# Gate projections ahead of the S5 output steps, and a second norm begun sooner with three up blocks

## The chip, the cores and the metric

The kernel runs on one core of one Trainium2 chip, as one launch. The metric is the device time of that launch in microseconds. Five engines work side by side, each through its own list of instructions in order: TensorE (PE in the profile; PEld is its loading of weights), VectorE (DVE), ScalarE (ACT), GpSimd (POOL) and SyncE (SP), which here only issues DMAs. They wait for one another by semaphores.

## The reference

One layer of a hybrid decoder trunk, in fp32: 256 prompt tokens and 8 x 4 decode tokens, 2048 features.

```python
mod = silu(c) @ W_ada + b_ada        # shift1, scale1, gate1, shift2, scale2, gate2
h = rmsnorm(x) * (1 + scale1) + shift1
q, k, v, g, a_lr, u = split(h @ W_in)
# GLA: 4 heads, dk 128, dv 256; log a = logsigmoid(a_lr W_a2 + b_a2) / 16
S_t = diag(a_t) S_{t-1} + k_t^T v_t;  o_t = q_t S_t;  o = headnorm(o) * silu(g)
# S5: 64 groups of 16 channels, a complex diagonal state of 64 per group
s_t = Abar s_{t-1} + Bbar u_t;  y_t = Re(C s_t) + D u_t
z = gelu(y) * sigmoid(gelu(y) @ W_glu + b_glu)
x = x + gate1 * (concat[o, z] @ W_out)
h = rmsnorm(x) * (1 + scale2) + shift2
x = x + gate2 * ((gelu(a') * g') @ W_down)   # [a' | g'] = causal conv3(h @ W_up), 5632 wide each
y = rmsnorm(x)                               # the final norm
```

The new GLA, S5 and convolution states are outputs too.

## The kernel before

All 288 tokens lie on the free axis (32 decode tokens, then 256 of the prompt), the features on the 128 partitions. A weight block of 128 x 1024 comes by SP's DMA queue into a `raw` buffer, of which there are ten. `split` makes two halves of it for precision: `wh`, a cast on ScalarE (L128), and `wl`, the remainder, a subtraction on VectorE (L130). `mm3` multiplies each 128 x 128 tile three times into one PSUM block `acc`: wh with the activations' high part (L145), wh with their low part (L146), wl with the high part (L147). `proj2(m)` is the second half (8 of 16 feature tiles, 24 matmuls) of output block m of the in-projection; VectorE adds it to the first half, which stands in SBUF.

The adaLN vectors (`mod`) are computed in units of 16 matmuls of 512 columns each (L197, `ada_mms`), straight from four raw buffers of the weight `wadf` each. `step(ada_b, 1)` and `step(ada_g2, 1)` put half a unit's work between other blocks; `chained` binds a unit's matmuls to one another and to `tail`, the last matmul of the block before. A scheduler sets the order of the instructions on every engine from the program's order, priorities (loads and splits run ahead) and data dependences; `after` adds an order by hand.

The stages on the time axis: adaLN and in-projection, S5 preparation, the projections m = 8 to 23 beside the chunked attention, the S5 outputs with the projections m = 24 to 31 (which hold g, the gate of the GLA output), the GLA state update, the GLU, the out-projection ("mixer blocks", `mixo`, `x2`), the second norm, then up projection, convolution and down projection, and the final norm.

**S5 outputs.** The state `st` holds every fourth token after a scan on POOL: a step of four operations (L725 to L728) for each, one behind the other. For each f of 0 to 7, `advance` makes the tokens between (two products into `q`, L678, and two additions into `st`, L679, on VectorE for even f and on POOL for odd). 48 small matmuls into two PSUM tiles follow (L880 with `MM` and `UU`, L882 with `st`), copies on ScalarE into `zt` (L885), four transposes (L888) and a copy on VectorE (L890). Then comes projection 24 + f, whose result VectorE adds to `PG` (L894).

**GLA state.** The prompt's state is formed by the matmuls L922 and stored from tile `S11` to `o_glap` (L924, POOL's queue). The decode states come in pieces by loads from `sgla` (L949, same queue) into `S10`, `S11` (S in the profile) and `MM`, and are multiplied with the queries (L954). S11 is free for its load when the store has landed, MM when the last S5 output has read its matrix.

**Second norm.** The squares of x are summed up in `ssq` beside the mixer blocks; two matmuls with ones add `ssq` and the last `sq` (L1095, L1096), `rms_rstd` makes the scale `rst` (L156 to L161). Then, for pieces of 1, 1, 2, 4, 4 and 4 of the 16 feature tiles, x is multiplied with `rst` (L1104, the last two pieces on POOL), the decode tokens get their shift (L1106), ScalarE writes the high part `hh` (L1111, L1112) and VectorE the low part `hl` (L1117, L1119). `up_mm2` runs the first two up blocks together, a feature tile at a time, as its pieces come (L1156 to L1158).

## Time and profile before

| what | value |
|---|---|
| three runs | 1476.24, 1483.79, 1479.89 us; median 1479.89 |
| the profiled execution | 1480.4 us; its span 1478.5 us |
| PE busy | 1407.0 us, 95% of the span |
| DVE, ACT, POOL busy | 910.8, 677.7, 346.5 us |
| PE idle between 330 and 430 us | 14.8 us in one wait, about 7 in smaller ones |
| PE idle between 592 and 606 us | 3.02, 1.01, 2.56, 0.70 us |
| moved by DMA | 317 MB, 214 GB/s on the mean |

Times in a trace count from the start of the span. In the prediction's rows from the timeline stand the start, the duration, the engine, the line, the operation, output <- inputs by the program's names (buffer numbers left out) and the count; in brackets the idle time of the engine before it and what ended it. In rows of stretches stand the bounds, the length, the busy time and number of instructions of PE, PEld, DVE, ACT and POOL, then the granted clock of PE (1.00 is full), the DMA's busy share and its GB/s. Matmuls overlap in the pipeline, so their starts tell their pace.

### The profile page before, as it was taken

The numbers are of one execution on the slowest core, as the hardware profiler recorded it, in microseconds if no ns is written. First come the engines' busy times: TensorE is split into PE (matmuls) and PEld (weight loads), VectorE is DVE, ScalarE is ACT, GpSimd is POOL, SyncE is SP. The second block draws the span as 40 slices with busy tenths as digits, with TensorE's granted clock in tenths as the row PEclk, the third lists the DMA queues.
The fourth block names the chain that finished last, engine by engine and source line by source line (L and its number), as shares of the span: only waits on it lengthen the run. The fifth ranks groups of instructions, "written<-read, shape, count | busy, mean of one in ns | idle before, by whom it ended". The sixth has DMA issues, their size and how long they took to land.

```text
span 1478.5 us, 28963 instructions
## 1 busy us (share of the span) xinstructions
PE 1407.0 (95%) x11546; PEld 1298.6 (88%) x11546; DVE 910.8 (62%) x1643; ACT 677.7 (46%) x1131; POOL 346.5 (23%) x618
## 2 busy tenths in 40 slices
PE   5999999995999999899999999999999999999996
PEld 4777777774778988789999999999999999999995
DVE  6866573582366856755665666565655665666557
ACT  4651254334344445544435543554345534553445
POOL 1126013496211001332103320232023301330121
PEclk9999999998999999899999999999999999999998
DMA  9977978882679776678444445544544454445432
GB/s 374 336 270 224 357 272 289 280 285 88 246 272 376 270 274 239 251 274 295 161 169 167 162 147 183 170 160 154 177 166 168 160 171 159 170 160 169 148 103 79
DMA packets 88727, 316.96 MB, mean 214 GB/s; under 512 B 10368, under 2 KB 10784, under 8 KB 88592
## 3 DMA queue, kind: packets, MB, share of 16 engines
q1 hardware_dynamic: 84240, 299.72, 58.1%
q0 software_dynamic: 4064, 14.81, 2.9%
q8 instruction: 91, 1.49, 0.4%
q10 hardware_dynamic: 288, 0.59, 0.1%
q14 instruction: 44, 0.36, 0.1%
HBM read 306.63 MB, written 8.45 MB: 213 GB/s over the span
## 4 chain that ended last, share of the span: by engine, by line
PE 71%; POOL 4%; DMA 2%; DVE 2%; issue 1%; ACT 0%; DVEq 0%; SPq 0%; POOLq 0%; ACTq 0%
PE acc L145 22%; PE acc L146 22%; PE acc L147 22%; PE ada L197 2%; POOL q L726 1%; POOL st L728 1%; POOL q L725 1%; POOL st L727 1%; DMA raw<-wup 1%; PE s L882 1%; DMA MM<-sgla 1%; DMA o_glap<-S 1%; DMA S<-sgla 0%; PE gl L954 0%; DVE S L1106 0%
## 5 line engine op out<-in xcount | busy, mean ns | idle before, releaser
L128 ACT CAST wh<-raw 128x1024 fp32r<-128x1024 f32 (+1 forms) x376 | 386.0, 1030 | 570.5 <-PE acc L146 510.8
L130 DVE TENSOR_TENSOR wl<-raw,wh 128x1024 fp32r<-128x1024 f32 (+1 forms) x376 | 458.8, 1222 | 278.6 <-ACT wh L128 264.9
L145 PE MATMUL acc<-hh,wh 128*128 128x288 f32 x1376 | 407.7, 296 | 0.0
L146 PE MATMUL acc<-hl,wh 128*128 128x288 f32 x1376 | 405.9, 295 | 0.0
L147 PE MATMUL acc<-hh,wl 128*128 128x288 f32 x1376 | 404.4, 294 | 0.0
L145 PEld LDWEIGHTS acc<-hh,wh 128*128 128x128 f32 x1376 | 257.8, 187 | 4.2 <-ACT up L1167 4.2
L147 PEld LDWEIGHTS acc<-hh,wl 128*128 128x128 f32 x1376 | 259.1, 188 | 0.0
L146 PEld LDWEIGHTS acc<-hl,wh 128*128 128x128 f32 x1376 | 258.3, 188 | 0.0
L1168 POOL COPY cvo<-up 128x16 f32<-128x16 f32 x88 | 101.7, 1156 | 591.7 <-ACT up L1166 591.7
L146 PE MATMUL acc<-ffhl,wh 128*128 128x288 f32 x704 | 208.1, 296 | 0.0
L147 PE MATMUL acc<-ffhl,wl 128*128 128x288 f32 x704 | 207.6, 295 | 0.0
L145 PE MATMUL acc<-ffhl,wh 128*128 128x288 f32 x704 | 207.1, 296 | 0.5 <-ACT ffhl L1198 0.2
L145 PE MATMUL acc<-h,wh 128*128 128x288 f32 x512 | 158.4, 310 | 2.2 <-DVE PG L612 1.2
L147 PE MATMUL acc<-h,wl 128*128 128x288 f32 x512 | 152.9, 301 | 2.7 <-DVE wl L130 2.7
L146 PE MATMUL acc<-h,wh 128*128 128x288 f32 x512 | 153.7, 301 | 1.4 <-DVE h L477 0.9
L146 PEld LDWEIGHTS acc<-ffhl,wh 128*128 128x128 f32 x704 | 132.7, 188 | 0.1
L145 PEld LDWEIGHTS acc<-ffhl,wh 128*128 128x128 f32 x704 | 131.8, 188 | 0.9 <-ACT ffhl L1198 0.5
L147 PEld LDWEIGHTS acc<-ffhl,wl 128*128 128x128 f32 x704 | 132.0, 188 | 0.0
L1044 DVE SCALAR_TENSOR_TENSOR x<-acc,mod,x 128x256 f32<-128x256 f32 x128 | 61.6, 481 | 101.6 <-PE acc L147 101.4
L145 PEld LDWEIGHTS acc<-h,wh 128*128 128x128 f32 x512 | 97.7, 191 | 23.4 <-issue 9.9
L197 PE MATMUL ada<-raw,cS 128*32 128x512 f32 (+1 forms) x832 | 101.3, 569 | 5.0 <-DMA raw<-wadf 3.0
L147 PEld LDWEIGHTS acc<-h,wl 128*128 128x128 f32 x512 | 97.5, 191 | 3.9 <-DVE wl L130 3.4
(416 smaller groups left out, 1963.6 us busy)
## 6 DMA issues: line engine op xcount, KB each, us to landing
raw<-wup SPq DMA_DIRECT2D x176, 512.0 KB, 3.6
raw<-wadf SPq DMA_DIRECT2D x128, 512.0 KB, 6.6
raw<-wdn SPq DMA_DIRECT2D x80, 512.0 KB, 3.5
raw<-wadb SPq DMA_DIRECT2D x48, 512.0 KB, 7.0
raw<-win SPq DMA_DIRECT2D x32, 512.0 KB, 5.7
raw<-winc SPq DMA_DIRECT2D x32, 512.0 KB, 5.5
raw<-wout SPq DMA_DIRECT2D x32, 512.0 KB, 7.8
raw<-wad SPq DMA_DIRECT2D x16, 512.0 KB, 8.9
```

The lines of the kernel that those rows point to most:

```text
L128: cast[0] = S.copy(wh, raw)
L130: V.tensor_sub(wl, raw, wh.bitcast(F32))
L145: T.matmul(ps, wh[:, ks], xh(k), start=first, stop=False)
L146: T.matmul(ps, wh[:, ks], xl(k), start=False, stop=False)
L147: tail[0] = T.matmul(ps, wl[:, ks], xh(k), start=False, stop=last).ins
L197: mms.append(lambda c=c, kc=kc_of(blk, j), raw=raw, c0=c0, first=first, last=last: T.matmul(ps[32 * c:32 * c + 32, 0:w], cS[:, kc, :], raw ...
L725: G.tensor_tensor(q1, prev, a8[:, 0], op=ALU.mult)
L726: G.tensor_tensor(q2, prevs, a8[:, 1], op=ALU.mult)
L727: G.tensor_tensor(cur, cur, q1, op=ALU.add)
L728: G.tensor_tensor(cur, cur, q2, op=ALU.add)
L1044: V.scalar_tensor_tensor(x2[:, m, ND:], ps[:, ND:], mod[:, vi, m, 0:1], x2[:, m, ND:], op0=ALU.mult, op1=ALU.add)
L1168: G.tensor_copy(cvo[:, m, 0:16].rearrange("p (b w) -> p b w", w=2), upd[:, :, 4:6])
```

## The change

The loop over f runs four steps further and is shifted: projections 24 to 27 come before the first S5 output (`s5_out`), and each output f stands behind projection 28 + f, as long as there is one. VectorE's `advance` is ordered behind the addition of the projection before it, and an output's first matmul behind the last matmul before it.

In the second norm one adaLN unit stands ahead of the sum of squares, which is bound to it; four stay behind. All scaling is on VectorE, in pieces of 1, 1, 2, 2, 2, 4 and 4. The weights of three up blocks are loaded and split ahead (their pool has four buffers, not two), and `up_mm_first` runs three blocks together, the third in a PSUM tile `gl`: for each feature tile the six matmuls with hh, then the three with hl. In the final norm two scratch tiles come from another pool.

```diff
-        def advance(eng, dst, src, srcs, fs, n):
+        def advance(eng, dst, src, srcs, fs, n, prev=None):
...
+                if prev is not None and w_ == 0:
+                    order_after(ins.ins, prev)
                 eng.tensor_tensor(dst, dst, q, op=ALU.add)
...
-        for f in range(8):
+        def s5_out(f):
             fs = slice(4 * f, 4 * f + 4)
             advance(G if f % 2 else V, ...
-                    fs, 31)
+                    fs, 31, None if f % 2 else gadd[0])
...
+                    if al_ == 0 and j == 0:
+                        order_after(mm0.ins, tail[0])
...
-            ps = proj2(24 + f)
-            V.tensor_add(proj_dst(24 + f), ps, proj_dst(24 + f))
-            step(ada_b, 1)
+        for f in range(8 + 4):
+            if f < 8:
+                ps = proj2(24 + f)
+                gadd[0] = V.tensor_add(proj_dst(24 + f), ps, proj_dst(24 + f)).ins
+                step(ada_b, 1)
+            if f >= 4:
+                s5_out(f - 4)
...
+        keep_tail[0] = True
+        step(ada_g2, 1)
+        keep_tail[0] = False
         psn = ps_gl()[:, 0:NT]
-        T.matmul(psn, ones, ssq, start=True, stop=False)
-        T.matmul(psn, ones, sq, start=False, stop=True)
+        for i, t in enumerate((ssq, sq)):
+            ins = T.matmul(psn, ones, t, start=(i == 0), stop=(i == 1))
+            order_after(ins.ins, tail[0])
+            tail[0] = ins.ins
...
-        parts = ((0, 1), (1, 1), (2, 2), (4, 4), (8, 4), (12, 4))
+        parts = ((0, 1), (1, 1), (2, 2), (4, 2), (6, 2), (8, 4), (12, 4))
...
-            (V if k0 < 8 else G).tensor_tensor(t, t, rst..., op=ALU.mult)
+            V.tensor_tensor(t, t, rst..., op=ALU.mult)
...
-    wpools.append(ctx.enter_context(tc.tile_pool(name="wspb", bufs=2)))
-    up_w = [[f() for f in load_w(a["wup"][i])] for i in range(2)]
-    step(ada_g2, 5)
+    wspb = ctx.enter_context(tc.tile_pool(name="wspb", bufs=4))
+    wpools[:] = [wspb] * 4 + [wspa] * 2
+    up_l = [load_w(a["wup"][i]) for i in range(3)]
+    up_w = [[None, None] for _ in range(3)]
+    for i, hf in ((0, 0), (1, 0), (2, 0), (0, 1), (1, 1), (2, 1)):
+        up_w[i][hf] = up_l[i][hf]()
+    wpools[:] = [wspb, wspa, wspb]
+    step(ada_g2, 4)
...
+        pss = [ps_acc(), ps_acc(), ps_gl()[:, 0:NT]]
         for k in range(KC):
-            for i in range(2):
+            ks = slice(k % 8 * P, (k % 8 + 1) * P)
+            for i in range(3):
                 wh, wl = up_w[i][k // 8]
                 T.matmul(pss[i], wh[:, ks], hh[:, k], start=(k == 0), stop=False)
-                T.matmul(pss[i], wh[:, ks], hl[:, k], start=False, stop=False)
-                T.matmul(pss[i], wl[:, ks], hh[:, k], start=False, stop=(k == KC - 1))
+                T.matmul(pss[i], wl[:, ks], hh[:, k], start=False, stop=False)
+            for i in range(3):
+                wh, wl = up_w[i][k // 8]
+                tail[0] = T.matmul(pss[i], wh[:, ks], hl[:, k], start=False, stop=(k == KC - 1)).ins
```

On VectorE, at the end of the attention and the first S5 output, before the change: the addition of the last v projection, a weight split, the four state operations of output 0, then the copies and additions of the next steps.

```order
L864 TENSOR_TENSOR PV_31_296<-acc_4176,PV_31_296 128x288
L130 TENSOR_TENSOR wl_4338<-raw_4246,wh_4336 128x1024
L678 TENSOR_TENSOR q_4202<-st,a_2335 128x248
L678 TENSOR_TENSOR q_4205<-st,a_2335 128x248
L679 TENSOR_TENSOR st<-st,q_4202 128x2x4x31
L679 TENSOR_TENSOR st<-st,q_4205 128x2x4x31
L915 TENSOR_TENSOR PT_802_4869<-gl_4894,PT_802_4869 32x512
L890 COPY UU_699_4242<-tr_4237 128x4x72
```

After it (L910 is the addition to PG, L684 and L687 are the state operations, L903 the copy):

```order
L910 TENSOR_TENSOR PG_32_297<-acc_4290,PG_32_297 128x288
L130 TENSOR_TENSOR wl_4368<-raw_4362,wh_4366 128x1024
L910 TENSOR_TENSOR PG_32_297<-acc_4336,PG_32_297 128x288
L130 TENSOR_TENSOR wl_4456<-raw_4364,wh_4454 128x1024
L910 TENSOR_TENSOR PG_33_298<-acc_4370,PG_33_298 128x288
L684 TENSOR_TENSOR q_4412<-st,a_2335 128x248
L684 TENSOR_TENSOR q_4415<-st,a_2335 128x248
L687 TENSOR_TENSOR st<-st,q_4412 128x2x4x31
L130 TENSOR_TENSOR wl_4532<-raw_4526,wh_4530 128x1024
L687 TENSOR_TENSOR st<-st,q_4415 128x2x4x31
L903 COPY UU_732_4452<-tr_4447 128x4x72
```

Five splits and five additions now stand between the last v projection and the state operations, and a split between the two additions into `st`.

On PE at the load into S11 (S_818; gl_4945 collects the decode tokens' outputs), before: the transposes of output 4 follow, and then a projection.

```order
L954 MATMUL gl_4945<-S_818_4951,PV_814_4933 32x256 x2
L954 MATMUL gl_4945<-S_817_4950,PV_814_4933 32x256 x2
L954 MATMUL gl_4945<-S_818_4951,PV_814_4933 32x256 x2
L880 MATMUL s_764_4629<-MM_1538,UU_473_2818 72x64
L888 MATMUL tr_4565<-ident,zt_4536 128x72 x4
L145 MATMUL acc_4580<-h_1807,wh_4576 128x288
```

After, with output 5 right behind them:

```order
L972 MATMUL gl_4945<-S_818_4951,PV_814_4933 32x256 x2
L972 MATMUL gl_4945<-S_817_4950,PV_814_4933 32x256 x2
L972 MATMUL gl_4945<-S_818_4951,PV_814_4933 32x256 x2
L891 MATMUL s_781_4747<-MM_1538,UU_473_2818 72x64
L901 MATMUL tr_4733<-ident,zt_4704 128x72 x4
L891 MATMUL s_782_4748<-MM_1538,UU_473_2818 72x64
L895 MATMUL s_781_4747<-cA,st 72x64 x2
```

No projection is left to stand between the outputs 4 to 7; they have all gone ahead. Before the last prompt-state matmul stand three outputs now, as before, but all but one of the projections.

On PE at the second norm, before (a unit is four of the rows L197, one for each raw buffer; the last row is the first up matmul):

```order
L197 MATMUL ada_6954<-raw_6955,cS 32x512 x2
L197 MATMUL ada_6954<-raw_6977,cS 32x512 x2
L197 MATMUL ada_6954<-raw_6975,cS 32x512 x2
L197 MATMUL ada_6954<-raw_6973,cS 32x512 x2
L1095 MATMUL gl_6853<-PT_914_5544,ones 128x288
L197 MATMUL ada_6954<-raw_6971,cS 32x512 x2
L1096 MATMUL gl_6853<-sq_6848,ones 128x288
L197 MATMUL ada_6954<-raw_6993,cS 32x512 x2
L197 MATMUL ada_6954<-raw_6991,cS 32x512 x2
L197 MATMUL ada_6954<-raw_6989,cS 32x512 x2
L197 MATMUL ada_6954<-raw_6987,cS 32x512 x2
L1156 MATMUL acc_7013<-hh,wh_6934 128x288
```

After:

```order
L203 MATMUL ada_6853<-raw_6854,cS 32x512 x2
L1117 MATMUL gl_6870<-PT_914_5544,ones 128x288
L1117 MATMUL gl_6870<-sq_6848,ones 128x288
L203 MATMUL ada_6853<-raw_6993,cS 32x512 x2
L203 MATMUL ada_6853<-raw_6991,cS 32x512 x2
L203 MATMUL ada_6853<-raw_6989,cS 32x512 x2
L203 MATMUL ada_6853<-raw_6987,cS 32x512 x2
L203 MATMUL ada_6853<-raw_7009,cS 32x512 x2
L203 MATMUL ada_6853<-raw_7007,cS 32x512 x2
L203 MATMUL ada_6853<-raw_7005,cS 32x512 x2
L203 MATMUL ada_6853<-raw_7003,cS 32x512 x2
L1184 MATMUL acc_7029<-hh,wh_6963 128x288
```

The sum of squares has moved ahead by nearly a unit; three units stand ahead of the first up matmul as before, two of them behind the sum.

More of the change, by code (lines that the diff above doesn't have):

```diff
@@ L137, in tile_hybrid_step @@
     tail = [None]
+    keep_tail = [False]
     def mm3(ps, w, xh, xl, nk, start, stop):
@@ L166, in after, with order_after @@
     def after(ins, prev):
-        tc.add_manual_dep(ins.ins, prev.ins.name, mybir.DependencyInfo(
+        order_after(ins.ins, prev.ins)
+    def order_after(ins, prev):
+        tc.add_manual_dep(ins, prev.name, mybir.DependencyInfo(
             mybir.DependencyClass.NoSync, mybir.DependencyReason.DATA), reason="order on the engine")
@@ L178, in chained @@
             last = ins.ins
+        if keep_tail[0]:
+            tail[0] = last
     def ada_mms(ps, w, blks, nblk, load, kc_of):
@@ L677, in advance @@
                     "p (r a c) -> p r a c", r=2, a=4)
-                eng.tensor_tensor(q, x, a4[:, w_, :, fs].unsqueeze(3).to_broadcast([P, 2, 4, n]), op=ALU.mult)
+                ins = eng.tensor_tensor(q, x, a4[:, w_, :, fs].unsqueeze(3).to_broadcast([P, 2, 4, n]), op=ALU.mult)
+                if prev is not None and w_ == 0:
+                    order_after(ins.ins, prev)
                 eng.tensor_tensor(dst, dst, q, op=ALU.add)
@@ L867, in tile_hybrid_step @@
         ybuf = []
-        for f in range(8):
+        gadd = [None]
+        def s5_out(f):
             fs = slice(4 * f, 4 * f + 4)
             advance(G if f % 2 else V, st[:, :, fs, NB + 3::2], st[:, :, fs, NB + 2:NCOL:2], st[:, ::-1, fs, NB + 2:NCOL:2],
-                    fs, 31)
+                    fs, 31, None if f % 2 else gadd[0])
             zt = t2k.tile([P, 512], F32, tag="t2k", name=nm("zt"))
@@ L879, in tile_hybrid_step @@
                     o = pzs[j][:, al_ * 64:(al_ + 1) * 64]
-                    T.matmul(o, ut[f][js, al_], mm_[js, pr], start=True, stop=False)
+                    mm0 = T.matmul(o, ut[f][js, al_], mm_[js, pr], start=True, stop=False)
+                    if al_ == 0 and j == 0:
+                        order_after(mm0.ins, tail[0])
                     for r in range(2):
@@ L1099, in tile_hybrid_step @@
         hl = epa.tile([P, KC, NT], F32R, tag="CA", name="hl")
-        parts = ((0, 1), (1, 1), (2, 2), (4, 4), (8, 4), (12, 4))
+        parts = ((0, 1), (1, 1), (2, 2), (4, 2), (6, 2), (8, 4), (12, 4))
         def n2_scale(k0, n):
             t = xa[k0 // 4][:, k0 % 4:k0 % 4 + n]
-            (V if k0 < 8 else G).tensor_tensor(t, t, rst.unsqueeze(1).to_broadcast([P, n, NT]), op=ALU.mult)
+            V.tensor_tensor(t, t, rst.unsqueeze(1).to_broadcast([P, n, NT]), op=ALU.mult)
             td = t[:, :, 0:ND]
@@ L1148, in up_mm, with up_mm_first @@
         return ps
-    def up_mm2(m):
-        pss = [ps_acc(), ps_acc()]
+    def up_mm_first():
+        pss = [ps_acc(), ps_acc(), ps_gl()[:, 0:NT]]
         for k in range(KC):
-            for i in range(2):
+            ks = slice(k % 8 * P, (k % 8 + 1) * P)
+            for i in range(3):
                 wh, wl = up_w[i][k // 8]
-                ks = slice(k % 8 * P, (k % 8 + 1) * P)
                 T.matmul(pss[i], wh[:, ks], hh[:, k], start=(k == 0), stop=False)
-                T.matmul(pss[i], wh[:, ks], hl[:, k], start=False, stop=False)
-                T.matmul(pss[i], wl[:, ks], hh[:, k], start=False, stop=(k == KC - 1))
+                T.matmul(pss[i], wl[:, ks], hh[:, k], start=False, stop=False)
+            for i in range(3):
+                wh, wl = up_w[i][k // 8]
+                tail[0] = T.matmul(pss[i], wh[:, ks], hl[:, k], start=False, stop=(k == KC - 1)).ins
         return pss
@@ L1182, in tile_hybrid_step @@
             if i == 0:
-                pss = up_mm2(0)
+                pss = up_mm_first()
                 ca = up_conv(0, pss[0])
@@ L1186, in tile_hybrid_step @@
             else:
-                ca = up_conv(2 * i, up_mm(2 * i))
+                ca = up_conv(2 * i, pss[2] if i == 1 else up_mm(2 * i))
                 step(ada_g2, 1)
@@ L1227, in tile_hybrid_step @@
     rst = ffp.tile([P, NT], F32, name="rst3")
-    rt1 = ffp.tile([P, NT], F32, name="rt1c")
-    rt2 = ffp.tile([P, NT], F32, name="rt2c")
+    rt1, rt2 = [sml2.tile([P, NT], F32, tag="ft", name=nm("rt")) for _ in range(2)]
     rms_rstd(psn, rst, rt1, rt2)
```

## The prediction

> **What bounds the kernel now.** I read the page's busy shares first, then the waits of TensorE, then the timeline of the two places that the change touches, and last the other engines there. The page:
>
> ```profile
> PE 1407.0 (95%) x11546; PEld 1298.6 (88%) x11546; DVE 910.8 (62%) x1643; ACT 677.7 (46%) x1131; POOL 346.5 (23%) x618
> ```
>
> TensorE (PE) is busy for 1407.0 us, 95% of a span of 1478.5 (the table above): no order of the same matmuls can win more than its 71 idle us and what it loses at a low clock. Two waits of PE between 330 and 430 us (total, times, longest), and ten microseconds of that stretch:
>
> ```profile
> PE s L882 <- DVE st L679: 14.8, 1, 14.8
> PE gl L954 <- DMA S<-sgla: 0.9, 1, 0.9
> ...
> 350.00:360.00 10.00, 5.13 (x57) 4.48 (x58) 2.50 (x5) 1.88 (x5) 9.17 (x20) 0.58 0.01 5
> ```
>
> The first S5 output step waits 14.8 us for VectorE's state addition L679. The granted clock (third number from the end) has fallen meanwhile: 0.58 on the mean of this stretch. Who is late is seen on POOL and DVE:
>
> ```profile
> 332.84 0.34 POOL L725 TENSOR_TENSOR q<-st,a 128x64 f32<-128x64 f32 x1
> 335.77 1.31 POOL L725 TENSOR_TENSOR q<-st,a 128x64 f32<-128x64 f32 x1
> 338.21 0.35 POOL L725 TENSOR_TENSOR q<-st,a 128x64 f32<-128x64 f32 x1
> 339.69 0.35 POOL L725 TENSOR_TENSOR q<-st,a 128x64 f32<-128x64 f32 x1
> ...
> 332.73 0.46 DVE L864 TENSOR_TENSOR PV<-acc,PV 128x288 f32<-128x288 f32 x1 [0.18 <-PE acc L147]
> 335.65 1.23 DVE L130 TENSOR_TENSOR wl<-raw,wh 128x1024 fp32r<-128x1024 f32 x1 [2.47 <-ACT wh L128]
> 352.87 0.90 DVE q L678 x2
> 354.87 0.75 PE L882 MATMUL s<-cA,st 64*72 64x64 f32 x8 [14.82 <-DVE st L679]
> 357.97 0.76 PE L906 MATMUL gl<-ident,PV 128*32 128x128 f32 x4
> ```
>
> POOL's serial scan (L725 to L728, 1.48 us a step from 338.21 to 339.69) ends at 352.85; VectorE's four state operations follow, and PE starts at 354.87. The weight split L130 stretches the scan operation beside it from 0.35 to 1.31 us; the addition out of PSUM at 332.73 leaves its neighbour at 0.34. The second place is the second norm:
>
> ```profile
> 586.32 3.63 PE L197 MATMUL ada<-raw,cS 128*32 128x512 f32 x28
> 591.54 0.75 PE L1096 MATMUL gl<-sq,ones 128*128 128x288 f32 x2
> 595.31 1.93 PE L197 MATMUL ada<-raw,cS 128*32 128x512 f32 x16 [3.02 <-DMA raw<-wadf]
> 598.25 0.53 PE L1156 MATMUL acc<-hh,wh 128*128 128x288 f32 x2 [1.01 <-ACT hh L1112]
> 601.34 0.61 PE L1157 MATMUL acc<-hl,wh 128*128 128x288 f32 x1 [2.56 <-DVE hl L1119]
> 605.28 0.61 PE L1157 MATMUL acc<-hl,wh 128*128 128x288 f32 x1 [0.70 <-DVE hl L1119]
> 610.73 0.38 PE L1156 MATMUL acc<-hh,wh 128*128 128x288 f32 x1
> ...
> 598.00:600.00 2.00, 0.53 (x2) 0.30 (x2) 1.97 (x2) 0.71 (x2) 2.00 (x1) 1.00 1.02 412
> 602.00:604.00 2.00, 2.00 (x10) 2.00 (x10) 1.98 (x4) 1.03 (x3) 0.00 (x0) 0.50 1.04 424
> 612.00:614.00 2.00, 2.00 (x18) 2.00 (x17) 0.85 (x1) 1.94 (x2) 0.38 (x2) 1.00 0.47 83
> ...
> 595.38 2.51 DVE L1106 TENSOR_TENSOR S<-S,mod 128x32 f32<-128x32 f32 x1
> 601.99 0.23 DVE L1106 TENSOR_TENSOR S<-S,mod 128x64 f32<-128x64 f32 x1
> 610.71 0.28 DVE L1119 TENSOR_TENSOR hl<-S,hh 128x128 fp32r<-128x128 f32 x1
> 594.95 5.79 POOL L1104 TENSOR_TENSOR S<-S,PT 128x1152 f32<-128x1152 f32 x2 [7.39 <-DVE PT L161]
> ```
>
> Three gaps follow one another; the last comes from VectorE's first two small additions, 2.5 us each beside POOL's large products where one of double size takes 0.23 later. The clock is still full at 598 to 600, but from 601.34 to 610.73 it is at half: ten matmuls ran in 602 to 604, eighteen in 612 to 614.
>
> **Part 1, the S5 outputs.** Five projections and three adaLN units now run on PE while the scan ends. One projection is the stretch between the first two of these rows, 3.3 us, an output step that between the second and third, 1.75; a unit is 1.9 (595.31):
>
> ```profile
> 369.24 0.47 PE L888 MATMUL tr<-ident,zt 72*128 72x72 f32 x4
> 372.88 0.27 PE L882 MATMUL s<-cA,st 64*72 64x64 f32 x1
> 374.63 0.70 PE L922 MATMUL gl<-PQ,S 128*128 128x256 f32 x2
> ```
>
> Five of the one and three of the other make 22.2 us; with some small transposes PE goes from 332.7 to about 356. The scan gets five splits beside it where one stood, four times 0.96 more, and ends at 356.7. VectorE's state operations take 1.95 us, and a split of 1.2 now stands between them: the first output starts at 359.8, some 1.5 us after PE's transposes in between. The 14.8 us are nearly gone. But 23 us of cover are spent, and what is late next is the GLA state:
>
> ```profile
> 375.17 0.59 PE L922 MATMUL gl<-PK,S 128*128 128x256 f32 x2
> 385.00 7.20 DMA S<-sgla
> 407.13 1.72 POOL L679 TENSOR_TENSOR st<-st,q 128x248 f32<-128x248 f32 x2 [3.80 <-PE s L882]
> 415.06 7.98 DMA MM<-sgla
> 423.08 0.63 PE L954 MATMUL gl<-MM,PV 128*32 128x256 f32 x4 [1.40 <-DMA MM<-sgla]
> ```
>
> The last prompt-state matmul ends at 375.8; the store o_glap (L924), the load that waits for it on POOL's queue and its landing take until 392.2, 16.4 us. After the change the same matmul ends at about 380.8 (first output 359.8, three outputs, two projections, a unit, the other small matmuls), so the load lands at 397.2. PE has one projection (3.3), two outputs and small matmuls for cover, until 391.2: it waits 6.0 us where it waited 0.9. Then outputs five to seven stand one behind another, each held by the additions into the state, half of DVE's 1.95 us or 1.72 on POOL, until 406.9. The load into MM waits for the last of them and lands 8.1 later at 415.05; eight GLU matmuls (1.1 us) are all the cover. That place stood at 423.08: at full clock this part wins 8.0 us. The gate projections' adds read PSUM like the one at 332.73, so I cost them at nothing to POOL. Behind VectorE's state operations, which now wait for the gate addition ahead of them, stand the next projection's split and the copy of the outputs; each comes a projection ahead of its use. Behind the S load on POOL stands output five's state work; PE waits for the load itself, so it costs nothing more.
>
> The clock takes much of it back. Before, 14.8 us of idling cost half clock until about 358 (the 350:360 row: 0.58), and the first output took 3.1 us (354.87 to 357.97) in place of 1.75. The 6 us at the load should do the same. Three outputs at half clock cost 3 x 1.35 = 4.0, delaying the MM load as much; the small gaps between them leave half clock on, as in 601.34 to 610.73. After the MM wait the next matmuls cost about 2.5 (between 1.7, half of 3.4 us as from 354.87 to 358.3, and 4.7, half of 9.4). Part 1 then nets 8.0 - 4.0 - 2.5 = 1.5 us; the ends are 8.0 and -0.7. I take 1.5, since the gaps look like those of the second norm.
>
> By the Trainium skill, "TensorE: Matmul & The Clock Gate", Part 1: The HAM clock gate, the clock halves after an idle window of about 3.4 us and comes back after as long a stretch of sustained work; the trace agrees at 354.87, but from 601.34 it took 9.4 us with one gap of 0.7. By the page alone the cold stretch at the outputs would cost an estimated 1.7 us, and part 1 would net about 4.
>
> **Part 2, the second norm.** One adaLN unit instead of nearly two stands ahead of the sum of squares, so its second matmul starts near 588.9 instead of 591.5 and the scale 1/rms is ready near 592.3 instead of 594.9, where POOL begins. With all scaling on VectorE, the two additions lose their 2.3 us each; two large products (1.35 us, as the next row shows) come to DVE. The last hl falls 16.1 - 4.6 + 2.7 = 14.2 us after the scale, at 606.5.
>
> ```profile
> 602.63 1.35 DVE L1104 TENSOR_TENSOR S<-S,PT 128x1152 f32<-128x1152 f32 x1
> 587.83 0.86 SPq L116 DMA_DIRECT2D raw<-wadf x2
> 646.55 1.85 PE ada L197 x16
> ```
>
> None of this starts the up blocks: units two and three stand ahead of their first matmul in PE's order. The third unit's loads wait for buffers that the first unit frees, as before, where the last two were issued from 587.83 and the unit began at 595.31. The first unit runs at the same time, so I keep 595.3, and the first up matmul comes at 597.2 (before 598.25; ends 594 and 600, if the loads land 3 us sooner or later). On SP the third up block's two loads now stand ahead of units two and three; unit two's loads come some microseconds later for it, and PE wants them at 589. Those two loads bring two splits of 1.23 us to VectorE during the last mixer blocks; at 62% busy it should cover them, and I take nothing (end: 2.5 us, none covered). Then nine matmuls for each k (1.2 us) run behind a production that leads by 4 us: the waits of 2.56 and 0.70 go, and so does the half clock (9.4 us less 0.7, and of that eight parts in eighteen: 3.9). From 598.25 to the adaLN unit at 646.55, from which the order is the same, were 48.3 us; 41.1 remain, and the unit comes at 638.3: 8.2 won. If the 3.7 us of idling before the third unit lower the clock, as the 3.0 before did not, up to 3.9 are lost again; I take 0.9. Part 2 nets 7.3, with ends at 11 and 0.3.
>
> **Part 3, the end.** The two scratch tiles of the last norm come from another pool; the chain of operations is the same. Cost nothing, no cover needed.
>
> **Sum.** 1.5 + 7.3 = 8.8. The profiled execution took 1480.4 us, the median of the runs is 1479.9: I forecast 1471.5, from 1468 to 1475 for this case.
>
> **Rivals.** (a) The clock stays full at both places: 8.0 + 8.2 = 16.2, about 1464. For it: 3.0 us of idling at 592 to 595 did not lower it. Against: 6.0 us are twice that. (b) The new waits eat the gain: half clock from the S5 load past the MM wait (-0.7), the unit's loads 3 us later and the old 9.4 us of half clock after them (8.2 - 3 - 3.9 = 1.3): 1480. For it: the last loads needed seven microseconds from issue to use already, and more stands ahead of them on SP now. Against: what stands ahead waits for splits that are done before the mixer ends. (c) It is slower, by the scan alone: when VectorE works without a break on operands in SBUF, a scan step takes not 1.48 but 4.2 us:
>
> ```profile
> 323.06 0.94 POOL L725 TENSOR_TENSOR q<-st,a 128x64 f32<-128x64 f32 x1
> 327.24 0.74 POOL L725 TENSOR_TENSOR q<-st,a 128x64 f32<-128x64 f32 x1
> ```
>
> Some 13 steps are left at 332.84. At 3.2 us each they last until 375, the first output starts 18 us later, everything behind it follows, and the time is 1489. The gain is gone from 2.5 us a step. Against it: VectorE has only five splits there, 6.1 of 23 us.
>
> **How the numbers follow.** Forecast 0.45, (a) 0.2, (b) 0.25, (c) 0.07, faster than (a) 0.03. A difference under 0.5% (7.4 us) can hardly be told from none. Faster by more means under 1472.5: two thirds of the forecast's share, (a) and the rest, 0.52; slower is (c) and a little of (b), 0.08; within 0.40. From 1463 to 1480 lie all but (c), the upper part of (b) and the fastest few.
>
> **What would show it.** Right: PE's wait for L679's successor under 3 us; a wait of 4 to 7 us on the S load and of 3 to 5 on the MM load, with half clock between them; the first up matmul at 9 to 12 us after the last mixer matmul, and no wait on hl. Wrong: scan steps over 2 us; a wait on hh or hl in the up blocks; a clock of 1.0 through the outputs (then faster), or of 0.5 after 605 in the up blocks.

## The result, and the profile after

The changed kernel takes 1464.05 us (median of four runs, 1462.54 to 1467.12), the kernel before 1478.07 us in the same series: a ratio of 0.9891, with a 95% interval of 0.9862 to 0.992. The forecast was 1471.5 us, from 1468 to 1475. The profiled execution of the changed kernel took 1467.12 us, its span 1465.3.

To compare stages, three marks are taken from each trace: the first operation of the S5 scan on POOL, an adaLN unit among the mixer blocks, and an adaLN unit among the up blocks. First the kernel before, from the timeline and from the chain that ended last:

```profile
287.20 0.36 POOL L725 TENSOR_TENSOR q<-st,a 128x64 f32<-128x64 f32 x1 [3.06 <-DVE st L679]
...
550.70 1.92 PE ada L197 x16
661.40 1.85 PE ada L197 x16
```

The same rows after:

```profile
289.81 0.35 POOL L733 TENSOR_TENSOR q<-st,a 128x64 f32<-128x64 f32 x1 [3.07 <-DVE st L687]
...
545.91 1.85 PE ada L203 x16
648.30 1.85 PE ada L203 x16
```

From the scan to the mixer (stage 1, the S5 outputs and the GLA state) the time fell from 263.5 to 256.1 us, from the mixer to the up blocks (stage 2, the second norm) from 110.7 to 102.4. From there to the end it is 817 us in both. The change lies behind the scan's start, but that start differs between executions (283.4 to 292.3 us in the traces of this study), here by 2.6 us to the disadvantage of the changed kernel: 7.4 + 8.3 - 2.6 = 13.1 us, the difference of the spans (13.2).

TensorE's waits and four stretches of the timeline of the S5 outputs, after (waits: total, times, longest; stretches: the third number from the end is the granted clock):

```profile
PE s L895 <- POOL s5p L738: 6.1, 1, 6.1
PE gl L972 <- DMA S<-sgla: 2.3, 1, 2.3
...
350.00:360.00 10.00, 7.82 (x63) 5.92 (x61) 2.21 (x3) 5.51 (x6) 9.06 (x25) 1.00 0.98 343
360.00:370.00 10.00, 6.12 (x59) 6.04 (x60) 3.67 (x6) 2.25 (x5) 6.79 (x12) 0.50 0.59 222
400.00:410.00 10.00, 9.57 (x118) 8.16 (x110) 2.75 (x6) 2.17 (x6) 1.58 (x3) 0.55 0.01 2
410.00:420.00 10.00, 8.32 (x69) 6.64 (x68) 5.00 (x10) 5.43 (x14) 2.17 (x4) 0.50 0.30 106
```

The wait of 14.8 us before the first output is 6.1 now, that for the S load 2.3, and the clock is at half behind both. There is no wait for the load into MM in this execution. The transfers of the GLA state, from the chain and the timelines of POOL and PE:

```profile
388.70 6.33 DMA o_glap<-S
395.62 4.12 DMA S<-sgla
...
414.42 1.12 POOL L967 DMA_DIRECT2D MM<-sgla  x2 [3.29 <-PE s L895]
...
418.81 1.07 PE L972 MATMUL gl<-MM,PV 128*32 128x256 f32 x4
```

S lands 4.12 us after its issue (7.20 before), MM is used 4.4 us after its issue (8.0 before), with no wait noted. The second norm:

```profile
585.16 1.92 PE L203 MATMUL ada<-raw,cS 128*32 128x512 f32 x16
590.78 1.92 PE L203 MATMUL ada<-raw,cS 128*32 128x512 f32 x16 [3.69 <-DMA raw<-wadf]
592.63 0.40 PE L1184 MATMUL acc<-hh,wh 128*128 128x288 f32 x1
...
598.00:600.00 2.00, 2.00 (x17) 2.00 (x16) 1.97 (x6) 1.43 (x4) 0.00 (x0) 1.00 1.02 391
602.00:604.00 2.00, 2.00 (x18) 2.00 (x17) 0.94 (x2) 1.79 (x2) 0.00 (x0) 1.00 0.27 102
...
588.32 0.19 DVE L1129 TENSOR_TENSOR S<-S,mod 128x32 f32<-128x32 f32 x1
```

No matmul waits for hh or hl any more, the clock stays at 1.0, and VectorE's small addition takes 0.19 us where it took 2.51. What is left is 3.69 us for the loads of the third adaLN unit.

### The profile page after: what moved, and what is told of

It reads as the page before. It is cut to its first block, busy times and chain, and to the rows that moved or that the text cites. A ratio compares the mean times of both kernels' runs of the same rounds, so it can differ in the third digit from the quotient of the medians.

```text
span 1465.3 us, 29026 instructions
## 1 busy us (share of the span) xinstructions
PE 1408.3 (96%) x11546; PEld 1301.8 (89%) x11546; DVE 908.1 (62%) x1648; ACT 676.8 (46%) x1132; POOL 343.5 (23%) x616
## 4 chain that ended last, share of the span: by engine, by line
PE 72%; POOL 5%; DMA 1%; DVE 1%; issue 1%; ACT 0%; DVEq 0%; POOLq 0%; ACTq 0%
PE acc L146 22%; PE acc L147 22%; PE acc L148 22%; PE ada L203 2%; POOL st L736 1%; POOL q L733 1%; POOL q L734 1%; POOL st L735 1%; PE s L895 1%; DMA raw<-wadf 0%; PE s L891 0%; DMA o_glap<-S 0%; PE gl L972 0%; PE acc L1184 0%; PE acc L1185 0%
## 5 line engine op out<-in xcount | busy, mean ns | idle before, releaser
L130 DVE TENSOR_TENSOR wl<-raw,wh 128x1024 fp32r<-128x1024 f32 (+1 forms) x376 | 458.2, 1221 | 274.6 <-ACT wh L128 261.7
L146 PE MATMUL acc<-hh,wh 128*128 128x288 f32 x1360 | 402.8, 296 | 0.0
L147 PE MATMUL acc<-hl,wh 128*128 128x288 f32 x1360 | 401.1, 295 | 0.0
L148 PE MATMUL acc<-hh,wl 128*128 128x288 f32 x1360 | 399.9, 294 | 0.0
L146 PEld LDWEIGHTS acc<-hh,wh 128*128 128x128 f32 x1360 | 254.7, 187 | 3.6 <-ACT up L1197 1.1
L148 PEld LDWEIGHTS acc<-hh,wl 128*128 128x128 f32 x1360 | 256.1, 188 | 0.0
L147 PEld LDWEIGHTS acc<-hl,wh 128*128 128x128 f32 x1360 | 255.1, 188 | 0.8 <-issue 0.8
```

Of the source, the lines that this page charges most:

```text
L130: V.tensor_sub(wl, raw, wh.bitcast(F32))
L146: T.matmul(ps, wh[:, ks], xh(k), start=first, stop=False)
L147: T.matmul(ps, wh[:, ks], xl(k), start=False, stop=False)
L148: tail[0] = T.matmul(ps, wl[:, ks], xh(k), start=False, stop=last).ins
```

## The experiments

The marks above, for each kernel's profiled execution (us; the stages are those named above), beside the medians of the runs and the ratio to the kernel before in the same series:

| kernel | scan begins | stage 1 | stage 2 | median | ratio, 95% interval |
|---|---|---|---|---|---|
| before | 287.2 | 263.5 | 110.7 | 1478.07 | |
| after | 289.8 | 256.1 | 102.4 | 1464.05 | 0.9891 (0.9862 to 0.992) |
| e1, part 1 alone | 285.4 | 255.2 | 109.9 | 1469.46 | 0.993 (0.9907 to 0.9952) |
| e2, part 2 alone | 283.4 | 264.8 | 105.2 | 1474.6 | 0.9973 (0.9958 to 0.9987) |
| e3, three projections ahead | 290.2 | 263.9 | 104.0 | 1475.42 | 0.9966 (0.9952 to 0.9979) |
| e4, five splits away | 284.1 | 252.9 | 105.8 | 1461.72, one run | |
| e5, extra stores of the outputs | 286.9 | 259.1 | 104.8 | 1470.02 | 0.9941 (0.9923 to 0.9958) |
| e6, scan's end on VectorE | 285.7 | 263.7 | 105.9 | 1471.77 | 0.9943 (0.9925 to 0.9962) |
| e7, two up blocks | 289.2 | 251.7 | 108.0 | 1466.44 | 0.9901 (0.9868 to 0.9934) |
| e8, upper half scaled on POOL | 285.1 | 254.1 | 104.0 | 1461.16 | 0.9881 (0.9848 to 0.9914) |
| e9, extra stores of a constant | 292.3 | 261.8 | 104.1 | 1474.41 | 0.9964 (0.9945 to 0.9983) |
| e10, filler at S | 285.7 | 254.0 | 105.7 | 1464.45 | 0.9901 (0.9876 to 0.9926) |
| e11, filler at S and unit three | 286.5 | 254.1 | 104.6 | 1462.51 | 0.9887 (0.987 to 0.9904) |
| e12, shorter filler | 289.8 | 253.8 | 102.8 | 1459.83 | 0.9861 (0.9838 to 0.9884) |

Stage 1 has the same code in the kernel after, e1, e7 and e8, and lies between 251.7 and 256.1 us: a single trace says no more than some 4 us there. In these four the spread goes with the clock: between 350 and 430 us TensorE stood at half clock for 31 us in the kernel after, 27 in e1, 24 in e8 and 14 in e7, and stage 1 took 256.1, 255.2, 254.1 and 251.7 us. The wait before the first output was 6.1, 4.5, 4.5 and 2.6 us in the same order.

### e1: part 1 alone

The kernel after with the second norm and the first up blocks of the kernel before.

> Only the S5 output part of the change, the second norm as before. In the changed kernel's trace the adaLN unit ahead of the mixer blocks' last half comes 4.8 us earlier than before (545.84 against 550.63), so this kernel should be 4 to 6 us faster than before, near 1473 us. Theory A: loads of the GLA state land sooner when no weights are being loaded beside them; here the S load should land about 4.1 us after its issue and the MM load about 4.4, as in the changed kernel, where 7.2 and 8.0 stood before. Rival B: those durations differ by chance from one execution to the next; then one of them may come out near 7 here.

1469.46 us: 10.4 less than before in the same series, where the expectation was 4 to 6. Stage 1 is as short as with both parts, stage 2 about as long as before. The part forecast at 1.5 us carries most of the gain. The S load landed 4.1 us after its issue and the one into MM was used after 4.3, as theory A expected; chance from one execution to the next (rival B) does not show.

### e2: part 2 alone

The kernel before with the new norm and the three up blocks.

> Only the second norm and the three up blocks, the S5 outputs as before. From the last mixer matmul to the first adaLN unit of the up blocks whose order is unchanged, the changed kernel took 8.2 us less than before; this kernel should be 7 to 9 us faster than before, near 1470 us, with the clock at 1.00 from the norm on. Theory A: the S5 outputs stand beside projections and weight loads again, so the S load should land 7 us and the MM load 8 us after its issue. Rival B: any value from 4 to 8.

1474.6 us: 5.3 less than before, where 7.3 were forecast and 7 to 9 expected. With the old order of the outputs the S load takes 8.0 us from issue to use and the one into MM 8.6, as theory A expected. PE waits 16.2 us for the first output, as before, and 4.4 us for the third unit's loads. Behind that wait (the granted clock is again the third number from the end):

```profile
592.00:594.00 2.00, 0.00 (x0) 0.00 (x0) 1.97 (x7) 1.23 (x5) 0.00 (x0) 1.00 1.01 377
594.00:596.00 2.00, 1.86 (x12) 0.59 (x16) 1.97 (x6) 1.05 (x4) 0.00 (x0) 0.58 1.02 420
...
598.00:600.00 2.00, 2.00 (x17) 2.00 (x16) 1.97 (x6) 1.30 (x4) 0.00 (x0) 1.00 1.04 422
```

The clock fell for 3.4 us, which it did not in the profile of the kernel after.

### e3: three projections ahead in place of four

```diff
-        for f in range(8 + 4):
+        for f in range(8 + 3):
...
-            if f >= 4:
-                s5_out(f - 4)
+            if f >= 3:
+                s5_out(f - 3)
```

> The changed kernel with a lead of three projections ahead of the first output instead of four. The first output still waits for the scan, so PE's wait there grows by one projection, from 6.1 to about 9.4 us, and one more projection stands between the outputs. Theory C (the half clock behind the first wait and the S wait is what the outputs five to seven pay): the S wait of 2.3 us goes, the clock stays full from 401 to 421, and about 6 us of half clock are saved: 3.3 - 2.3 - 6 = 5 us faster than the changed kernel, near 1459. Rival D (cover alone counts): 3.3 - 2.3 = 1 us slower than the changed kernel, near 1465.

1475.42 us, slower than the kernel after by some 11 us; both expectations missed it. Its waits, and VectorE's rows around the fifth output's state operations:

```profile
PE s L895 <- POOL s5p L738: 7.2, 1, 7.2
PE gl L972 <- DMA S<-sgla: 3.2, 1, 3.2
PE s L895 <- DVE st L687: 3.1, 1, 3.1
...
403.08 0.46 DVE L910 TENSOR_TENSOR PG<-acc,PG 128x288 f32<-128x288 f32 x1 [4.09 <-PE acc L148]
403.46 0.73 DVE L684 TENSOR_TENSOR q<-st,a 128x248 f32<-128x248 f32 x2
...
404.65 1.22 DVE L130 TENSOR_TENSOR wl<-raw,wh 128x1024 fp32r<-128x1024 f32 x1
...
406.42 0.41 DVE L687 TENSOR_TENSOR st<-st,q 128x248 f32<-128x248 f32 x1
```

The third wait is new. The last projection now comes after the S load; the state operations behind its addition (that is what the ordering of `advance` does) start only at 403.46, with a split between the two additions, so the fifth output waits, and all outputs behind it. They then run at half clock (0.50 from 410 to 420 us), and the load into MM is issued 133.0 us after the scan's start, where the kernel after needs 124.6. With one projection less ahead, nothing of stage 1's gain is left; how much of that loss comes from the ordering of `advance` alone was not tried. This kernel also bears on the landing times: four weight loads were issued on SP's queue at 390.4 us, at the same time as the S load (DMA share 0.81), and it took 6.4 us; the load into MM, with a share of 0.61, took 4.3.

### e4: no low part for five projections

For projections 24 to 28 the split returns the high part in place of the low one, so VectorE does no L130 for them.

> The changed kernel with the five splits beside the scan left out: projections 24 to 28 use the high part of their weights in place of the low part, so their VectorE subtraction is missing and the matmuls stay the same in number. Theory E (the scan on POOL, held by the splits, sets the first output): the scan ends about five times 1.0 us earlier, PE's wait before the first output falls from 6.1 to about 1 us and the clock stays full there; the mixer's adaLN unit comes 5 to 8 us earlier than in the changed kernel (545.8). Rival F (the split between VectorE's two state additions sets it): the wait stays at 5 us or more.

1461.72 us in one run. PE no longer waits for the scan (0.4 us are left), whose first thirty steps take 65.4 us (65.6 before) where the kernel after takes 70.8: about one microsecond for each split. The clock stays at 1.0 until the S load. Yet stage 1 is only 3 us shorter than in the kernel after, which is within the spread of one code. Counted from the scan's start, the first output comes 2.3 us sooner and not 6.1, since PE itself comes to it later, and S is there 4.6 us sooner; the wait of 2.9 us for S and the half clock behind it (390 to 410 us) remain.

### e5: extra stores of the outputs beside the GLA loads

```diff
             ybuf.append(yb)
+            for _ in range({2: 2, 6: 2}.get(f, 0)):
+                scr = dram.tile([P, 8, NT], F32, name=nm("scr"))
+                nc.sync.dma_start(scr, yb.unsqueeze(1).to_broadcast([P, 8, NT]))
```

> The kernel after, with two extra stores of 1.18 MB each to a scratch tensor behind the copy of output two (they run while o_glap is stored and the GLA state S is loaded) and two behind that of output six (beside the load into MM); nothing reads them. Theory A: these landings are short after the change because no weight loads run beside them. Then S lands in 6.5 to 8 us again (4.1 after) and MM in 7 to 9 (4.4), PE waits 5 to 7 us at S and 1 to 3 at MM, and the kernel takes 1469 to 1473 us, near the forecast. Rival B: the landings are short for another reason (their place in POOL's queue, what is written ahead of them); then they stay at 4 to 5 us and the time at 1463 to 1466.

1470.02 us, and the load into MM took 9.0 us from its issue at 407.53 to its use at 416.52. But the S load landed 5.2 us after its issue, less than the 6.5 to 8 expected, and PE did not wait for it; PE waited 4.4 us for ScalarE, which waited itself:

```profile
394.37 0.44 ACT L1003 ACTIVATE UU<-UU 128x288 f32<-128x288 f32 x1 [4.23 <-DMA scr<-UU]
```

ScalarE overwrites the output in place, and the extra stores still read it. The time fits theory A, but a part of it is this wait, so the experiment was made again as e9.

### e6: the last ten scan steps on VectorE

```diff
+            E = V if c >= 45 else G
-            G.tensor_tensor(q1, prev, a8[:, 0], op=ALU.mult)
+            E.tensor_tensor(q1, prev, a8[:, 0], op=ALU.mult)
...
```

> The kernel after, with the last ten steps of the S5 scan on VectorE in place of POOL. Theory F: POOL's 1.48 us a step and the splits beside it set the first output, and VectorE has room for ten steps of 0.8 to 0.9 us. Then the wait before the first output falls from 6.1 us to under 1.5, the clock stays full there, and 5 to 8 us are won on the kernel after: 1456 to 1460. Rival G: on VectorE the steps stand between splits that PE needs, PE waits for weights or for the scan as long as before, 1463 to 1468. Theory H: the first output comes 6 us sooner, but the S load then has that much less cover behind it, so the gain moves into the wait on S: 1461 to 1463.

1471.77 us, slower than the kernel after; above all three expectations. The wait before the first output is gone, but another took its place (waits of PE, and VectorE's timeline):

```profile
PE gl L774 <- DVE S L811: 9.4, 1, 9.4
...
334.63 0.27 DVE L734 TENSOR_TENSOR q<-st,a 128x64 f32<-128x64 f32 x1 [10.99 <-POOL st L737]
```

The first of the ten steps stands on VectorE ahead of an operation of the attention (L811) and waits there 11 us for POOL's step before it; PE's attention matmuls wait for L811. That is rival G's kind of wait, longer than it was priced. How much the scan's end on VectorE would win from a better place in its list was not tried.

### e7: two up blocks

```diff
-    up_l = [load_w(a["wup"][i]) for i in range(3)]
+    up_l = [load_w(a["wup"][i]) for i in range(2)]
...
-            for i in range(3):
+            for i in range(2):
```

> The kernel after, with two up blocks in the first group as before, the rest of the new norm kept. Theory: six matmuls for each k (0.8 us) run faster than the norm produces; at k=8 (some 598.5 us) the low part of hh is not there before 601, so a wait of 2 to 3 us on hl comes back, perhaps with half clock behind it: 1466 to 1470. Rival: the sooner norm alone made the gain, no wait of over 0.5 us on hl, 1463 to 1465.

1466.44 us, whose interval covers the kernel after. In stage 2, though, only 2.7 of the 8.3 us are left (108.0 against 102.4 us): waits for hl and hh came back, and half clock with them.

```profile
PE acc L1188 <- DVE hl L1142: 1.5, 3, 0.8
...
PE acc L1184 <- ACT hh L1135: 0.9, 1, 0.9
```

So the third block is worth 5.6 us beside the kernel after and 2.1 to 4.0 beside the other kernels with three blocks and no filler (104.0 to 105.9 us), and nothing that the runs show; the waits came as the theory said, smaller than it said, and its price in time is not shown.

Stage 1, whose code is unchanged, was 4.4 us shorter in this trace. Its stretches show less half clock than those of the kernel after (0.55 and 0.50):

```profile
400.00:410.00 10.00, 7.25 (x132) 6.40 (x130) 3.01 (x6) 4.44 (x12) 3.73 (x6) 0.94 0.06 17
410.00:420.00 10.00, 9.23 (x50) 6.83 (x50) 6.87 (x16) 2.71 (x8) 0.54 (x1) 0.66 0.39 144
```

The half clock behind the S load (a wait of 2.0 us here) lasted 3.4 us and not 20. From the fifth output's transposes to the eighth's it took 11.9 us, where the kernel after took 15.0. PE then waited 0.8 us for the load into MM, and the clock fell there.

### e8: the upper half of the norm scaled on POOL again

```diff
-            V.tensor_tensor(t, t, rst.unsqueeze(1).to_broadcast([P, n, NT]), op=ALU.mult)
+            (V if k0 < 8 else G).tensor_tensor(t, t, rst.unsqueeze(1).to_broadcast([P, n, NT]), op=ALU.mult)
```

> The kernel after, with the scaling of the upper half of the norm on POOL again (k from 8), the rest kept. Theory: VectorE's first two small additions take some 2.5 us each again beside POOL's products, the low part of k=1 to 3 comes 2 to 4 us later, PE waits 1 to 3 us on hl soon after the first up matmul: 1465 to 1469. Rival: the slack of the three blocks covers it, 1463 to 1465.

1461.16 us, no slower than the kernel after, and below both ranges. The mechanism came back (VectorE and POOL):

```profile
581.70 2.48 DVE L1129 TENSOR_TENSOR S<-S,mod 128x32 f32<-128x32 f32 x1
584.58 2.50 DVE L1129 TENSOR_TENSOR S<-S,mod 128x32 f32<-128x32 f32 x1
...
581.27 5.77 POOL L1127 TENSOR_TENSOR S<-S,PT 128x1152 f32<-128x1152 f32 x2 [3.68 <-DVE PT L162]
```

but PE waits for nothing that VectorE makes there: the third unit's wait and the three blocks cover it. As the rival says, PE does not feel it. All scaling on VectorE is not what made the gain, as far as four runs tell.

### e9: extra stores of a constant beside the GLA loads

```diff
             ybuf.append(yb)
+            if f in (2, 6):
+                scr = dram.tile([P, 10, 510], F32, name=nm("scr"))
+                V.tensor_copy(tg[:, 0:1], yb[:, 0:1])
+                nc.sync.dma_start(scr[:, 0, 0:1], tg)
+                nc.sync.dma_start(scr, vec[:, 0:510].unsqueeze(1).to_broadcast([P, 10, 510]))
```

> The kernel after, with one extra store of 2.6 MB from a constant to a scratch tensor behind the copy of output two (beside the store o_glap and the S load) and one behind that of output six (beside the load into MM); each is started by a store of one column that VectorE copies from the output. Nothing waits for these stores and nothing reads what they write; e5 read a tile that ScalarE later wrote over, and ScalarE waited 4.2 us for it. Theory A (other transfers in the DMA engines set the landing times): o_glap and the S load take 2 to 4 us longer together, the MM load 7 to 9 us from issue to use (4.4 after); PE waits 4 to 7 us at S and 1 to 4 at MM; 1468 to 1472 us, near the forecast. Rival B (the landings are short for another reason): landings and waits as after, 1463 to 1466.

1474.41 us, an interval that lies wholly above that of the kernel after. Issues on POOL and first uses on PE:

```profile
395.98 0.53 POOL L973 DMA_DIRECT2D S<-sgla  x1 [6.47 <-DMA o_glap<-S]
...
406.45 1.92 PE L978 MATMUL gl<-S,PV 128*32 128x256 f32 x12 [5.16 <-DMA S<-sgla]
...
417.57 1.12 POOL L973 DMA_DIRECT2D MM<-sgla  x2 [3.29 <-PE s L896]
...
428.76 0.62 PE L978 MATMUL gl<-MM,PV 128*32 128x256 f32 x4 [1.83 <-DMA MM<-sgla]
```

S took 10.5 us from issue to use and MM 11.2, where they take 4.1 and 4.4 without the stores; PE waits 5.2 and 1.8 us. Beside these transfers only two copies of one column were added. Theory A holds, and with more traffic than the kernel before had there (its stretches show a DMA share of 0.88 and 0.99, this one 1.05) stage 1 takes 261.8 us: nearly all of its gain is gone. By the Trainium skill, "DMA: Bandwidth & Descriptors", Issuing engines are not separate DMA queues, transfers started by different engines run on the same sixteen DMA engines and interleave; the stores of SP's queue and the loads of POOL's agree with it here.

### e10 and e11: filler matmuls where PE waits

```diff
+    def fill(n, prev, ps):
+        for i in range(n):
+            w_ = T.matmul(ps[:, 0:256].rearrange("p (c s) -> p c s", s=32), ident, cS[:, 0:8, :],
+                          start=(i == 0), stop=(i == n - 1))
+            order_after(w_.ins, prev)
+            prev = w_.ins
+        return prev
...
+            if f == 4:
+                warm[0] = fill(10, sm.ins, ps_acc())
...
+    step(ada_g2, 2)
+    tail[0] = fill(14, tail[0], ps_acc())
+    step(ada_g2, 2)
```

The last three lines are in e11 alone. The first matmul that needs the loaded S and the first of output five are ordered behind the filler.

> The kernel after, with ten matmuls of two constants (0.23 us each at full clock, into a PSUM tile that nothing reads) behind output four's last matmul, where PE waits 2.3 us for the S load. Theory K: that wait lets the clock fall at about 401 us, and three outputs and the first GLU matmuls then run at half clock until 421 us; with the gap filled the clock stays at 1.0 and the outputs, bound by PE at half clock (4.5 us each), come 1 to 1.5 us sooner each: 4 to 6 us won on the kernel after, 1458 to 1460. Rival L: the gaps between the outputs (0.2 to 1.7 us) let the clock fall all the same, or the outputs are bound by the additions into the state and not by PE: 1463 to 1466.

> As e10, and fourteen more such matmuls between the second and the third adaLN unit ahead of the up blocks, where PE waits 3.7 to 4.4 us for the third unit's loads. Theory M: in six of the seven profiles with the new norm and three up blocks that wait was followed by 2 to 7 us of half clock; filled, the clock stays full in the first up matmuls, 1 to 3 us won on e10: 1455 to 1458 if K holds, 1461 to 1464 if only this part holds. Rival N: the filler delays the third unit or changes nothing: as e10 within 1 us.

e10 takes 1464.45 us and e11 1462.51, both with intervals that cover the kernel after. The clock did what K says until 409 us, but the time is the one that L named; e10's stretches:

```profile
390.00:400.00 10.00, 10.00 (x129) 8.30 (x127) 1.91 (x4) 2.86 (x7) 3.10 (x5) 1.00 0.25 88
400.00:410.00 10.00, 7.49 (x126) 5.97 (x126) 3.72 (x7) 5.17 (x15) 3.73 (x6) 0.99 0.14 32
```

But the filler was sized wrongly: a row counts two records for each of these fp32 matmuls, so one takes 0.46 us and not 0.23.

```profile
392.23 4.58 PE L177 MATMUL acc<-cS,ident 128*128 128x256 f32 x20
```

Ten lasted 4.58 us where PE had waited 2.3, and fourteen 6.3 where it had waited 3.7. Stage 1 is 254.0 and 254.1 us, within the spread of the code without filler: what the clock gave, the filler seems to have taken. In e11 the clock stayed at 1.0 through the whole norm.

### e12: shorter filler

Six in place of ten, eight in place of fourteen.

> As e11, with six filler matmuls at the S load in place of ten and eight ahead of the third unit in place of fourteen. In e11 a filler matmul took 0.45 us and not 0.23, so they lasted 4.6 us where PE had waited 2.3, and 6.3 where it had waited 3.7. Theory: the clock stays at 1.0 at both places, outputs and up blocks start 1.8 and 2.5 us sooner than in e11: 1457 to 1460 us. Rival: six are too few and the clock falls at S or in the up blocks, 1461 to 1465.

1459.83 us, as the theory said and the lowest median of the study, at a ratio of 0.9861 (0.9838 to 0.9884) to the kernel before. The interval still touches that of the kernel after, so a gain on it is likely and not shown. Its profiled execution was the slowest of its four runs (1465.43), with the scan's start at 289.8 us. PE, in the norm and at the outputs:

```profile
585.05 3.72 PE L177 MATMUL acc<-cS,ident 128*128 128x256 f32 x16
589.22 1.93 PE L211 MATMUL ada<-raw,cS 128*32 128x512 f32 x16 [0.46 <-DMA raw<-wadf]
...
400.00:410.00 10.00, 8.96 (x167) 7.08 (x164) 3.45 (x7) 2.61 (x7) 2.61 (x4) 1.00 0.01 2
```

The clock is full in both places; it falls later, behind a wait of 0.9 us for the load into MM (0.50 from 415 to 420 us). From the fifth output's transposes to the eighth's it takes 11.2 us (401.05 to 412.27) where the kernel after took 15.0 (401.04 to 416.04): half clock costs some 3.8 us at these outputs. In e7 the same stretch was 3.2 us shorter without any filler, so a clock that stays nearly full there can come by chance; in the three traces with filler it was full until 409 us or later.

## Why the prediction was too small

**Part 1: forecast 1.5 us, 7.4 by the traces, 10.4 by the runs of e1.** The trace after has the longest stage 1 of the four with this code; their mean is 254.3 us, against 264.2 for the two with the old one (before and e2), which makes 9.9. All places below are given on the time axis of the kernel before, 2.6 us less than in the trace after.

- The scan. Forecast: four more splits cost 0.96 us each, the first output starts at 359.8 after a wait of 1.5. Measured: it starts at 361.3 after 6.1. The first thirty steps grew by 5.1 us: 4.2 behind the seventeenth step, where the four further splits stand, and 0.9 ahead of it, where the code is the same (e7 shows nothing there, e1 0.7). A fifth split stretches the last step. Two of the stretched operations:

```profile
347.24 1.42 POOL L735 TENSOR_TENSOR st<-st,q 128x64 f32<-128x64 f32 x1
...
362.26 1.21 POOL L736 TENSOR_TENSOR st<-st,q 128x64 f32<-128x64 f32 x1
```

  The mechanism was right, the start 1.5 us off. The wait was off by more, since PE came to it at 355.2, some 3 us sooner than I had counted. It also let the clock fall (0.50 from 360 to 370 us), which had no term in the sum. Both errors point the wrong way for the result; the gain was larger all the same.
- The S load. "[T]he store o_glap (L924), the load that waits for it on POOL's queue and its landing take until 392.2, 16.4 us." These 16.4 us were added to 380.8, where the last prompt-state matmul was to end, "so the load lands at 397.2". This is the step that failed first. The matmul ended at 384.9, but store, load and landing took 12.2 us, so S landed at 397.1: the forecast place, by luck, from two errors that cancel. PE, itself later by then, waited 2.3 us and not 6.0.
- The outputs at half clock. Forecast 4.0 us; measured 3.8 (against e12). The half clock came as forecast, behind the wait at S; e7 shows that it need not last through the outputs.
- The MM load. "The load into MM waits for the last of them and lands 8.1 later." It was issued at 411.8, 0.9 later than forecast (406.9 and 4.0), and used 4.4 us later: 3.7 us won. So MM's matmuls stand 6.9 us sooner than before, where 4.0 were forecast. The wait that was to stand here did not come, and with it fell most of the term "[a]fter the MM wait the next matmuls cost about 2.5": the outputs' half clock ended some 2.7 us behind MM's first use (0.62 on the mean of 420 to 422 us), which can cost 1.3. Behind MM's matmuls 0.5 us more was won where 2.5 were to be lost. These two steps, 2.9 and 3.0 us, are the difference between 1.5 and 7.4.

The common cause is one reading. The two durations were taken from rows in which weight loads ran beside the transfer, and the change moves these very weight loads away. Beside S came those of the last projection, which now stands ahead of that load, and of an adaLN unit; beside MM came four of the GLU's, issued at 412.3 us in the trace before and at 380.8 in the one after. The stretches with the transfers, first before (S, MM), then after (DMA share: the number before the last):

```profile
385.00:392.20 7.20, 6.31 (x81) 5.51 (x80) 2.79 (x5) 3.20 (x5) 2.50 (x4) 1.00 0.88 354
415.00:423.00 8.00, 5.00 (x39) 4.78 (x39) 6.63 (x15) 7.38 (x16) 1.12 (x2) 1.00 0.99 390
...
395.60:399.80 4.20, 1.86 (x50) 1.71 (x49) 0.68 (x1) 1.77 (x4) 3.16 (x5) 1.00 0.47 157
414.40:418.80 4.40, 2.75 (x12) 2.41 (x12) 3.13 (x6) 3.88 (x11) 1.12 (x2) 0.50 0.59 200
```

The landings follow this traffic in e1, e2 and e3 as well. e9 puts traffic back with hardly anything else changed, and stage 1 goes from 256.1 to 261.8 us: 1.7 less than before. That this is so near the forecast's 1.5 is chance, since both landings took some 3 us longer there than the forecast had them, and traces of one code differ by 4 us.

**Part 2: forecast 7.3 us, 8.3 by the trace after, 5.3 by the runs of e2.** The full-clock sum was right: 8.2 forecast, 8.3 measured in the one profile where the clock stayed full. From the first up matmul to the adaLN unit 41.1 us were forecast and 40.8 measured (592.63 to 633.45); the third unit's wait is 3.69. The mis-sized term is the chance of half clock, taken as 0.9 us. Of nine profiles with the new norm, three blocks and nothing in that gap, eight show a fall behind it, for 3.4 us in five and 6.8 in three; their stage 2 is 104.9 us on the mean, 2.5 more than the kernel after. 8.3 less 2.5 is 5.8, near e2's 5.3. One of the named reasons was not needed: the small additions at 2.3 us each came back in e8 and cost nothing that could be measured.

**Rivals.** (a) named the time, 1464, by luck: the clock did not stay full at the outputs. (b) and (c) did not come; the wait for the third unit's loads was the one that (b) needed, and it grew by 0.7 us only. Of what would show each step, the waits before the first output (under 3 us, 6.1 came), for S (4 to 7, 2.3 came) and for MM (3 to 5, none came) were missed; half clock between, the first up matmul 11 us after the last mixer matmul and no wait on hl were seen. Scan steps over 2 us, named as a sign of being wrong, came where a split stood beside them (2.4 to 2.6 us), as the forecast's own 0.96 for a split implies.

**What stays open.** What the third up block is worth alone (e7: some us of a trace, nothing that the runs show), whether e12 beats the kernel after, and why the half clock behind the S load lasted 20 us in three traces of one code and 3.4 in the fourth.

## What to carry to other kernels

A landing time read from a trace belongs to the traffic beside it: before it goes into a sum, ask whether the change moves that traffic, and take the nearest row without it as the other bound. A short wait of TensorE can cost more than itself where work with gaps follows it, and some matmuls of constants, about as long as the wait, kept the clock there (e12); that they also win time is not shown. When serial work is moved to a faster engine, look at what is queued there behind its first instruction.

## What the runs showed of the hardware that was not expected

- The load of 512 KB into S and the two into MM took 4.1 and 4.4 us with little traffic beside them, 7.2 and 8.0 beside weight loads, and 10.5 and 11.2 beside a store of 2.6 MB on SP's queue.
- Every stretch of half clock in the S5 outputs and the norm of these traces lasts a multiple of some 3.4 us: 3.4 or 6.8 us behind the norm's wait of 3.7 to 4.4, with gapless matmuls; at the outputs, with gaps of 0.2 to 1.7 us, 20.5 in the kernel after, e1, e4, e8 and e9, but 3.4 in e7.
- A wait of 2.3 us was enough to bring the clock to half at the outputs, while one of 3.7 us in the norm left it at 1.0 in the kernel after and lowered it in e3 and e9 with the same code there. By the Trainium skill, "TensorE: Matmul & The Clock Gate", Part 1: The HAM clock gate, a free-running window of activity decides; that fits a fall that comes or does not come for the same gap, but the 2.3 us are less than the window of about 3.4 us that the page gives.
- One VectorE split beside POOL's scan costs 1.0 us, whichever of the four operations it meets: four of them behind the seventeenth step cost 4.1 to 4.2 us in the kernel after, e1, e7 and e8.
